# Activation rows of 272 instead of 266 floats in a float32r matmul stream: one inference step of a hybrid decoder trunk

## The chip, the cores and the metric

The kernel runs on one core of one Trainium2 chip. The metric is the device time of one execution in microseconds (us). A single profiled execution of the kernel before is at hand, and all durations of single instructions come from it.

## The reference

One decoding step of a two-layer trunk of width 2048 runs for 256 prompt tokens and 8 sample tokens together, 264 columns in all. Layer 0 mixes tokens by causal pooling over windows of 2, 4, 8 and 16; layer 1 by gated linear attention with four heads. Each mixer and each MLP ends in a layer norm over the residual:

```
x = layer_norm(alpha * x + mixer(x))          # pooling in layer 0, gated linear attention in layer 1
h = square(relu(x @ w1 + b1))                 # 2048 -> 8192
x = layer_norm(alpha * x + (h @ w2 + b2))     # 8192 -> 2048
...
proj = x @ w_in                               # layer 1: k, q, v and output gate, 48 blocks of 128 columns
y = (o * rsqrt(mean(o * o)) * norm_w * silu(og)) @ w_out
```

Outputs are the two groups' rows after the second layer, and the new pooling and attention states. All data are float32.

## The kernel before, in words

Activations lie transposed: 128 features on the partitions, and 264 tokens (`N`) along the free axis, so that the 2048 features make 16 tiles (`KT`). For accuracy, each float32 activation and each weight is split into a high part, rounded to the type float32r, and a low part, the rest. A product is then three float32r matmuls, issued by `mm3`: high weight by high activation (line 146), high weight by low activation (line 147), low weight by high activation (line 148). Two columns more (`NX` = 266) hold the gain and bias of a layer norm where a matmul takes them along, so that the norm can be applied after it.

The work is 320 units of weights: 128 for the MLP of each layer (four blocks, each of 16 units of `w1` and 16 of `w2`), 48 for `w_in`, 16 for `w_out`. A unit is a 128 x 2048 block of weights that gives one output tile. `stage` loads a unit by SP's DMA queue, two units ahead of its use; ScalarE casts it to the high part (line 133) and VectorE subtracts to get the low part (line 134). `project` then runs over the 16 activation tiles k, with three matmuls each, 48 in a row into one PSUM bank. TensorE's order is the program's order; between units small pieces of attention and norm work are slipped in by `slot`.

The activations of a stage are held by an object of the class `Parts`. Its 16 tiles are kept in eight pairs; a pair's high parts are one SBUF tile `hh` of 2 rows of `NX` floats in each partition, its low parts one tile `hl` of the same shape. Activation tile k is row k % 2 of pair k // 2. So `fresh` makes rows of 266 floats, 1,064 bytes, and hands out whole rows. Two sets of 16 such tiles exist, "a" and "b" (the method `hslot`); in the MLPs the stage of `w1` reads one and the stage of `w2` the other. In the compiled program of the kernel before the 32 slots lie 2,144 bytes apart (2 x 1,064, rounded up to a multiple of 32), from byte 38,912 of each partition on. In set "a" `hh` and `hl` slots alternate; in set "b" eight `hh` slots come before eight `hl` slots. The 128 x 128 weight blocks that the matmuls hold start at multiples of 512 bytes.

`Norm.__init__` lets GpSimd write the two extra columns (its lines 205 and 206 in the kernel before). In layer 1, head 0 has two tiles of its own, `k0` and `q0`, whose place is later taken by the high parts of the gated output of head 0; the other heads use slots of a set.

Of the kernel before, what the change touches and what calls it, by code (L numbers as in the profile page):

```python
# [6 lines left out]
F32 = mybir.dt.float32  # L7
F32R = mybir.dt.float32r
U8 = mybir.dt.uint8
AF = mybir.ActivationFunctionType  # L10
ALU = mybir.AluOpType
PSUM = bass.MemoryType.PSUM

P = 128
# [3 lines left out]
NS = 8  # L18
N = NP + NS
NX = N + 2  # L20
DFF = 8192
NBLK = DFF // D
HEADS = 4
# [28 lines left out]
def _body(ctx, tc, nc, a, o, stop):  # L52
    V, S, PE, G = nc.vector, nc.scalar, nc.tensor, nc.gpsimd
# [9 lines left out]
    def wtile():  # L63
        return work.tile([P, N], F32, name="wt")

    def bank(tag):
        return misc.tile([P, 512], F32, name=tag, bufs=2 if tag == "ma" else 1)
# [15 lines left out]
    def hslot(s, i, shape, dt, name):  # L83
        return hp.tile(shape, dt, name=name, tag=f"{s}{i}")

    class Parts:
        def __init__(self, s, pairs=range(8)):
            self.s = s
            self.hi, self.lo = [None] * KT, [None] * KT
            self.pairs = {}  # L90
            for i in pairs:
                self.fresh(i)

        def fresh(self, i, th=None):
            if th is None:
                th = hslot(self.s, i, [P, 2, NX], F32R, "hh")
            tl = hslot(self.s, 8 + i, [P, 2, NX], F32R, "hl")
            self.pairs[i] = th, tl
            for e in range(2):
                self.hi[2 * i + e], self.lo[2 * i + e] = th[:, e], tl[:, e]  # L100

        def pair(self, m):
            return self.pairs[m // 2]
# [34 lines left out]
    def next_unit():  # L138
        u = state["use"]
        state["use"] += 1  # L140
        while state["next"] < min(u + 1 + AHEAD, len(units)):
            stage()
        return ready.pop(u)
# [9 lines left out]
    def slot():  # L153
        for e in list(pending):
            e[0] -= 1
            if e[0] <= 0:
                pending.remove(e)
                e[1]()
        for chain in list(background):
            if next(chain, "done") == "done":  # L160
                background.remove(chain)
# [4 lines left out]
    def project(x, ncol=N):  # L166
        w = next_unit()
        ps = acc.tile([P, NX], F32, name="ps")
        for k in range(KT):
            c = slice((k % 8) * P, (k % 8 + 1) * P)  # L170
            hi, lo = w[k // 8]
            mm3(ps[:, :ncol], hi[:, c], lo[:, c], x.hi[k][:, :ncol], x.lo[k][:, :ncol], k == 0, k == KT - 1)
            if k % 4 == 3:
                slot()
        return ps
# [14 lines left out]
    class Norm:  # L190
        def __init__(self, name, x, ahead=1):
            self.g, self.b = name.replace("_", "_g"), name.replace("_", "_b")
            self.x = x
            self.ahead = ahead
            self.shifted = 8
            self.n = 0
            self.met = 0
            self.done = 0
            self.sd, self.sq, self.c = lnm, lnq, lnr
            if x is not None:  # L200
                at = OFF[self.g]
                gb = par[:, at:at + 2 * KT].rearrange("p (c m) -> p m c", c=2)
                for m in range(0, KT, 2):
                    hi, lo = x.pair(m)
                    G.tensor_copy(hi[:, :, N:], gb[:, m:m + 2])
                    G.tensor_tensor(lo[:, :, N:], gb[:, m:m + 2], hi[:, :, N:].bitcast(F32), op=ALU.subtract)

        def add(self, ps, scale=1.0):
            m = self.n
# [109 lines left out]
    def settle(ps, rows=P):  # L319
        col = work.tile([P, 2], F32, name="col")  # L320
        t = wtile()
        V.tensor_scalar(col[:rows], ps[:rows, N:NX], -1.0, None, ALU.mult)
        V.tensor_tensor(t[:rows], ps[:rows, :N], lnr[:rows], op=ALU.mult)
        V.scalar_tensor_tensor(t[:rows], lnm[:rows], col[:rows, 0:1], t[:rows], ALU.mult, ALU.add)
        return t[:rows], col[:rows, 1:2]

    def mlp(l, norm, x, h, nxt):
        later(2, norm.stats)
        for b in range(NBLK):
            for m in range(KT):  # L330
                bias = prm(f"b1_{l}", b * KT + m)
                if b == 0:
                    t, col = settle(project(x, NX))
                    V.tensor_tensor(col, bias, col, op=ALU.subtract)
# [23 lines left out]
    def gla(gctx, norm, xp, x, hg):  # L358
        gp = gctx.enter_context(tc.tile_pool(name="gp", bufs=1))
# [30 lines left out]
        def gate_low():  # L390
            ps = bank("mc")[:, :NX]
            for j in range(4):
                for e, part in enumerate((xp.hi, xp.lo)):
                    for g in range(4):
                        k = 4 * j + g
                        PE.matmul(ps[32 * g:32 * g + 32], lhsT=wg[:, 32 * k:32 * k + 32], rhs=part[k].bitcast(F32),
                                  start=j == 0 and e == 0, stop=j == 3 and e == 1, tile_position=(0, 32 * g))
            t, col = settle(ps)
            V.tensor_scalar(low, t, col, None, ALU.subtract)
# [24 lines left out]
        class Head:  # L424
            def __init__(self, h):
                self.h = h
                self.la = LA[:, 2 * h:2 * h + 2]
                self.pre = self.la[:, :, :NP]
                if h:
                    self.k = hslot(hg, 2 * h, [P, 2, N], F32, "k")  # L430
                    self.q = hslot(hg, 2 * h + 1, [P, 2, N], F32, "q")
                else:
                    self.k = gp.tile([P, 2, N], F32, name="k0")
                    self.q = gp.tile([P, 2, N], F32, name="q0")
                self.vtok = None
                self.oT = ZT[:, (8, 12, 0, 4)[h]:(8, 12, 0, 4)[h] + 4]
                self.turned = 0
                self.attended = self.sampled = self.normed = False
                self.lag = {}
# [256 lines left out]
        gated = Parts(hg, ())  # L696
# [23 lines left out]
        for h in range(HEADS):  # L720
            for t in range(4):
                ps = project(x)
                while not heads[h].normed:
                    slot()
                if t == 0:
                    for e in range(2):
                        gated.fresh(2 * h + e, gp.tile([P, 2, NX], F32R, name="kq"[e] + "0") if h == 0 else None)
                heads[h].gate(t, ps, gated)
        assert not background and not pending
        return gated  # L730
# [84 lines left out]
    with ExitStack() as gctx:  # L815
        xr = Parts("b")
        gated = gla(gctx, ln, ln.x, xr, "a")
        for m in range(KT):
            S.mul(Z[m], xr.hi[m][:, :N].bitcast(F32), ALPHA)
            V.scalar_tensor_tensor(Z[m], xr.lo[m][:, :N].bitcast(F32), ALPHA, Z[m], ALU.mult, ALU.add)  # L820
        xs = Parts("b")
        tc.keep_in_program_order(S.preload_act_table(AF.Abs_reciprocal_sqrt))
        ln = Norm("mix_1", xs)
        for m in range(KT):
            ln.add(project(gated))
# [10 lines left out]
def layout(i):  # L836
# [23 lines left out]
    tiles = lambda w, n: c(w.reshape(KT, P, n, P).transpose(2, 1, 0, 3)).reshape(n, P, D)  # L860
    r["w1"] = np.stack([tiles(w, DFF // P) for w in i["mlp_w1"]])
    r["w2"] = c(i["mlp_w2"].reshape(2, NBLK, KT, P, KT, P).transpose(0, 1, 4, 3, 2, 5)).reshape(2, NBLK, KT, P, D)
# [61 lines left out]
```

## Time and profile before

| | |
|---|---|
| median of 3 runs | 2081.34 us (2079.74 to 2082.94) |
| the profiled execution | 2082.59 us, of which its span from first to last instruction 2080.8 us |
| TensorE clock granted, mean over the span | 0.995 of 2.4 GHz |
| matmul records on TensorE | 16436, of them 15360 of `mm3` |

A row of the profile gives the line of the kernel, the engine (PE is TensorE, PEld its weight load, DVE VectorE, ACT ScalarE, POOL GpSimd, SP the queue of loads), the operation, the tiles written and read, shapes, count, busy time in us and the mean duration in ns. Matmuls overlap in the array, so the duration of one (285 ns) is longer than the distance between the starts of two. That distance, called pitch below, is what a row of matmuls costs.

### The profile page before, as it was taken

What the parts mean: (1) busy time and instruction counts of PE and PEld (TensorE: products, weight loads), DVE (VectorE), ACT (ScalarE), POOL (GpSimd) and SP (SyncE); (2) the same over time, 40 slices, a digit from 0 to 9 for tenths busy, and PEclk for the clock granted to TensorE, in tenths of its full rate; (3) what the DMA queues carried; (4) which work ended last, traced back from release to release, by engine and by line L of the source; (5) the groups of instructions that cost most, each with busy time, mean ns of one, the idle gap of its engine ahead of it and who ended that gap; (6) DMA issues with size and microseconds to landing.
All of it is one profiled execution on the core that took longest, in us unless ns stands there. A gap on an engine that the chain in (4) does not pass through costs nothing.

```text
span 2080.8 us, 38806 instructions
## 1 busy us (share of the span) xinstructions
PE 2055.9 (99%) x16436; PEld 2018.4 (97%) x16436; DVE 1254.3 (60%) x1969; ACT 1082.0 (52%) x1650; POOL 54.9 (3%) x130
## 2 busy tenths in 40 slices
PE   8999999999999999999999999999999999999996
PEld 8999999999999999998899999999999999999996
DVE  3976444444444458986778758865444444444465
ACT  3657355345435545856656645566454345435543
POOL 0000000000000000011111010000000000000000
PEclk9999999999999999999999999999999999999998
DMA  6554555554455554477676444545555455554442
GB/s 239 193 186 175 175 180 183 183 177 175 177 182 183 182 175 171 153 253 256 237 267 237 161 172 175 178 171 180 182 183 180 174 176 180 183 182 177 174 177 83
DMA packets 67470, 386.19 MB, mean 186 GB/s; under 512 B 7808, under 2 KB 12160, under 8 KB 25808
## 3 DMA queue, kind: packets, MB, share of 16 engines
q1 hardware_dynamic: 61232, 363.28, 49.9%
q0 software_dynamic: 5920, 20.28, 2.6%
q8 instruction: 128, 2.10, 0.4%
q14 instruction: 46, 0.38, 0.1%
q10 hardware_dynamic: 144, 0.16, 0.0%
HBM read 362.65 MB, written 22.14 MB: 185 GB/s over the span
## 4 chain that ended last, share of the span: by engine, by line
PE 94%; DVE 3%; ACT 1%; DMA 1%; SPq 0%; issue 0%; ACTq 0%; DVEq 0%
PE ps L146 30%; PE ps L148 30%; PE ps L147 30%; PE ma L469 1%; DVE wlo L134 1%; PE mb L638 1%; PE ma L567 1%; DMA xt<-in_xt 0%; PE ps L774 0%; ACT whi L133 0%; PE mc L624 0%; DMA raw<-in_w 0%; PE ma L523 0%; SPq L746 0%; DMA s<-in_st 0%
## 5 line engine op out<-in xcount | busy, mean ns | idle before, releaser
L147 PE MATMUL ps<-hl,whi 128*128 128x264 f32 (+1 forms) x5120 | 1460.7, 285 | 0.0
L146 PE MATMUL ps<-hh,whi 128*128 128x264 f32 (+1 forms) x5056 | 1454.0, 288 | 0.0
L148 PE MATMUL ps<-hh,wlo 128*128 128x264 f32 (+1 forms) x5056 | 1443.1, 285 | 0.0
L134 DVE TENSOR_TENSOR wlo<-raw,whi 128x1024 fp32r<-128x1024 f32 x640 | 783.5, 1224 | 606.9 <-ACT whi L133 604.6
L133 ACT CAST whi<-raw 128x1024 fp32r<-128x1024 f32 x640 | 671.0, 1049 | 857.9 <-PE ps L147 832.6
L147 PEld LDWEIGHTS ps<-hl,whi 128*128 128x128 f32 x5120 | 968.7, 189 | 3.7 <-issue 1.4
L146 PEld LDWEIGHTS ps<-hh,whi 128*128 128x128 f32 x5056 | 953.7, 189 | 16.5 <-issue 15.8
L148 PEld LDWEIGHTS ps<-hh,wlo 128*128 128x128 f32 x5056 | 955.4, 189 | 0.0
L179 DVE TENSOR_TENSOR hl<-wt,hh 128x264 fp32r<-128x264 f32 x188 | 79.9, 431 | 15.5 <-ACT hh L178 9.8
L350 DVE TENSOR_TENSOR zt<-zt,ps 128x264 f32<-128x264 f32 x96 | 41.2, 429 | 65.7 <-PE ps L148 65.6
L178 ACT CAST hh<-wt 128x264 fp32r<-128x264 f32 x188 | 76.7, 410 | 7.4 <-DVE wt L661 3.2
L339 ACT ACTIVATE wt<-wt 128x264 f32<-128x264 f32 x128 | 54.4, 425 | 3.9
L627 DVE SCALAR_TENSOR_TENSOR s<-mc,k,s 128x512 f32<-128x512 f32 x64 | 45.8, 744 | 3.4 <-PE mc L624 3.4
L338 ACT ACTIVATE wt<-ps,par 128x264 f32<-128x264 f32 x96 | 45.6, 475 | 0.0
L211 DVE SCALAR_TENSOR_TENSOR zt<-ps,zt 128x264 f32<-128x264 f32 x48 | 20.7, 431 | 38.9 <-PE ps L148 38.9
L607 ACT ACTIVATE s<-s,sa 128x512 f32<-128x512 f32 x64 | 42.7, 713 | 2.6 <-DMA s<-in_st 2.6
L628 POOL DMA_DIRECT2D out_ngs<-s x64 | 34.7, 542 | 351.0 <-DVE s L627 343.3
L253 ACT ACTIVATE wt<-zt 128x264 f32<-128x264 f32 x60 | 23.4, 411 | 17.0 <-DVE zt L211 17.0
L774 PE MATMUL ps<-px,pw 128*128 128x264 f32 x128 | 30.9, 402 | 0.0
L774 PEld LDWEIGHTS ps<-px,pw 128*128 128x128 f32 x128 | 25.3, 200 | 4.4
L302 ACT ACTIVATE wt<-zt,par 128x264 f32<-128x264 f32 x48 | 27.4, 601 | 1.1 <-DVE zt L301 1.1
L246 ACT ACTIVATE hh<-zt,par 128x264 fp32r<-128x264 f32 x48 | 24.1, 511 | 5.6 <-DVE zt L237 3.6
(181 smaller groups left out, 897.3 us busy)
## 6 DMA issues: line engine op xcount, KB each, us to landing
raw<-in_w SPq DMA_DIRECT2D x256, 1024.0 KB, 4.8
raw<-in_win SPq DMA_DIRECT2D x48, 1024.0 KB, 5.0
s<-in_st SPq DMA_DIRECT2D x64, 256.0 KB, 5.5
out_ngs<-s POOLq DMA_DIRECT2D x64, 256.0 KB, 3.0
raw<-in_wout SPq DMA_DIRECT2D x16, 1024.0 KB, 4.8
pw<-in_pw SPq DMA_DIRECT2D x4, 1024.0 KB, 9.9
xt<-in_xt SPq DMA_DIRECT2D x3, 768.0 KB, 8.8
out_y<-zt SPq DMA_DIRECT2D x8, 264.0 KB, 2.2
```

Source lines behind the costliest of these rows:

```text
L133: S.copy(hi, src)
L134: V.tensor_tensor(lo, src, hi.bitcast(F32), op=ALU.subtract)
L146: PE.matmul(ps, lhsT=whi, rhs=xh, start=start, stop=False)
L147: PE.matmul(ps, lhsT=whi, rhs=xl, start=False, stop=False)
L148: PE.matmul(ps, lhsT=wlo, rhs=xh, start=False, stop=stop_)
L178: S.copy(x.hi[m][:, :N], src)
L179: V.tensor_tensor(x.lo[m][:, :N], src, x.hi[m][:, :N].bitcast(F32), op=ALU.subtract)
L338: S.activation(t, project(x)[:, :N], AF.Relu, bias=bias)
L339: S.activation(t, t, AF.Square)
L607: S.mul(s0s[b][hf], s0s[b][hf], sa[:, 2 * h + hf, b:b + 1])
L627: V.scalar_tensor_tensor(s0, vb, self.k[:, hf, NP + b:NP + b + 1], s0, ALU.mult, ALU.add)
L774: PE.matmul(ps[:, :N], lhsT=w[:, c], rhs=px[2 * g + k // 2][:, k % 2], start=k == 0, stop=k == 3)
```

## The change

Rows of the pair tiles get 272 floats (1,088 bytes) instead of 266 (1,064), and the first 266 of each are used as before. The same is done to the two tiles of head 0, as `k0` and `q0` and as high parts of the gated output. No instruction is added or removed, and all shapes of reads and writes stay; only addresses change.

```diff
+NROW = 272
...
         def fresh(self, i, th=None):
             if th is None:
-                th = hslot(self.s, i, [P, 2, NX], F32R, "hh")
-            tl = hslot(self.s, 8 + i, [P, 2, NX], F32R, "hl")
+                th = hslot(self.s, i, [P, 2, NROW], F32R, "hh")
+            tl = hslot(self.s, 8 + i, [P, 2, NROW], F32R, "hl")
             self.pairs[i] = th, tl
             for e in range(2):
-                self.hi[2 * i + e], self.lo[2 * i + e] = th[:, e], tl[:, e]
+                self.hi[2 * i + e], self.lo[2 * i + e] = th[:, e, :NX], tl[:, e, :NX]
...
-                    G.tensor_copy(hi[:, :, N:], gb[:, m:m + 2])
-                    G.tensor_tensor(lo[:, :, N:], gb[:, m:m + 2], hi[:, :, N:].bitcast(F32), op=ALU.subtract)
+                    G.tensor_copy(hi[:, :, N:NX], gb[:, m:m + 2])
+                    G.tensor_tensor(lo[:, :, N:NX], gb[:, m:m + 2], hi[:, :, N:NX].bitcast(F32), op=ALU.subtract)
...
-                    self.k = gp.tile([P, 2, N], F32, name="k0")
-                    self.q = gp.tile([P, 2, N], F32, name="q0")
+                    self.k = gp.tile([P, 2, NROW], F32, name="k0")[:, :, :N]
+                    self.q = gp.tile([P, 2, NROW], F32, name="q0")[:, :, :N]
...
-                        gated.fresh(2 * h + e, gp.tile([P, 2, NX], F32R, name="kq"[e] + "0") if h == 0 else None)
+                        gated.fresh(2 * h + e, gp.tile([P, 2, NROW], F32R, name="kq"[e] + "0") if h == 0 else None)
```

## Rows read from the trace of the kernel before

**Rows 1.** The page's busy times: us, share of the span, instructions.

```profile
PE 2055.9 (99%) x16436; PEld 2018.4 (97%) x16436; DVE 1254.3 (60%) x1969; ACT 1082.0 (52%) x1650; POOL 54.9 (3%) x130
```

**Rows 2.** The chain that ended last, shares of the span by engine and line.

```profile
PE 94%; DVE 3%; ACT 1%; DMA 1%; SPq 0%; issue 0%; ACTq 0%; DVEq 0%
PE ps L146 30%; PE ps L148 30%; PE ps L147 30%; PE ma L469 1%; DVE wlo L134 1%; PE mb L638 1%; PE ma L567 1%; DMA xt<-in_xt 0%; PE ps L774 0%; ACT whi L133 0%; PE mc L624 0%; DMA raw<-in_w 0%; PE ma L523 0%; SPq L746 0%; DMA s<-in_st 0%
```

**Rows 3.** Busy time by stretch; the first lies inside the first MLP.

```profile
300.00:700.00 400.00, 400.00 (x3258) 400.00 (x3258) 195.20 (x204) 186.01 (x243) 0.00 (x0) 1.00 0.51 179
...
900.00:1100.00 200.00, 199.41 (x1544) 181.25 (x1544) 148.34 (x313) 121.11 (x213) 27.63 (x51) 1.00 0.74 258
```

**Rows 4.** TensorE's groups, shapes kept apart (the columns are the page's).

```profile
L147 PE MATMUL ps<-hl,whi 128*128 128x264 f32 x4480 | 1277.7, 285 | 0.0
L146 PE MATMUL ps<-hh,whi 128*128 128x264 f32 x4416 | 1268.5, 287 | 0.0
...
L146 PE MATMUL ps<-hh,whi 128*128 128x266 f32 x640 | 185.5, 290 | 0.0
...
L146 PE MATMUL ps<-q,whi 128*128 128x264 f32 x32 | 9.2, 287 | 0.0
```

**Rows 5.** Timeline of TensorE, a unit of 264 columns, line 147, tiles k = 0 to 8.

```profile
297.36 0.28 PE L147 MATMUL ps<-hl,whi 128*128 128x264 f32 x1
...
297.72 0.29 PE L147 MATMUL ps<-hl,whi 128*128 128x264 f32 x1
...
298.10 0.28 PE L147 MATMUL ps<-hl,whi 128*128 128x264 f32 x1
...
298.47 0.28 PE L147 MATMUL ps<-hl,whi 128*128 128x264 f32 x1
...
298.84 0.29 PE L147 MATMUL ps<-hl,whi 128*128 128x264 f32 x1
...
299.20 0.28 PE L147 MATMUL ps<-hl,whi 128*128 128x264 f32 x1
...
299.57 0.28 PE L147 MATMUL ps<-hl,whi 128*128 128x264 f32 x1
...
299.94 0.28 PE L147 MATMUL ps<-hl,whi 128*128 128x264 f32 x1
...
300.31 0.28 PE L147 MATMUL ps<-hl,whi 128*128 128x264 f32 x1
```

**Rows 6.** The same for a unit of 266 columns, k = 0 to 6.

```profile
1346.67 0.29 PE L147 MATMUL ps<-hl,whi 128*128 128x266 f32 x1
...
1347.05 0.28 PE L147 MATMUL ps<-hl,whi 128*128 128x266 f32 x1
...
1347.41 0.29 PE L147 MATMUL ps<-hl,whi 128*128 128x266 f32 x1
...
1347.78 0.29 PE L147 MATMUL ps<-hl,whi 128*128 128x266 f32 x1
...
1348.16 0.28 PE L147 MATMUL ps<-hl,whi 128*128 128x266 f32 x1
...
1348.53 0.28 PE L147 MATMUL ps<-hl,whi 128*128 128x266 f32 x1
...
1348.90 0.29 PE L147 MATMUL ps<-hl,whi 128*128 128x266 f32 x1
```

**Rows 7.** One line of `mm3` over the whole run: count, shortest/median/longest, first and last start.

```profile
L147 PE MATMUL ps<-hl,whi x5120: 278/285/389, 64.3 to 2061.5; 128*128 128x264 f32 x173, 128*128 128x266 f32 x24
```

**Rows 8.** The page's groups that write the pair tiles, and its loads of weights.

```profile
L179 DVE TENSOR_TENSOR hl<-wt,hh 128x264 fp32r<-128x264 f32 x188 | 79.9, 431 | 15.5 <-ACT hh L178 9.8
...
L178 ACT CAST hh<-wt 128x264 fp32r<-128x264 f32 x188 | 76.7, 410 | 7.4 <-DVE wt L661 3.2
...
raw<-in_w SPq DMA_DIRECT2D x256, 1024.0 KB, 4.8
```

## The prediction

> **What bounds the kernel now.** I read the page's busy times first, for which engine could set the end: TensorE is busy for 99% of the span, VectorE for 60%, ScalarE for 52%, GpSimd for 3% [rows 1]. The chain of work that ended last says the same from the other side: 94% of it is TensorE, and lines 146, 147 and 148, the three matmuls of `mm3`, hold 30% each [rows 2]. Then the stretches, to see whether any part of the run is bound otherwise. Inside the first MLP TensorE has no idle time at all in 400 us, while VectorE works 195 and ScalarE 186 of them; in attention, where the other engines have most to do, VectorE reaches 148 of 200 us and TensorE still stands at 199.4 [rows 3]. So the time is the pitch of TensorE's matmuls, from start to start, times their number. In the first MLP that is 400 us / 3258 = 122.8 ns [rows 3]. The granted clock there is 1.00, which is 2.4 GHz, so 264 columns at one column a cycle would take 110 ns. Some 12.8 ns of each pitch, a tenth of the run, is something else, and the change can only act there: it adds no instruction, it moves operands.
>
> **What the addresses are.** A row of 1,064 bytes is 66.5 times 16. A pair tile starts at a multiple of 32, so activation tile k starts on a multiple of 16 where k is even and 8 bytes past one where k is odd. With 1,088 bytes (17 times 64) and slots of 2,176 (34 times 64) from byte 38,912 (a multiple of 64), every row of every pair starts at a multiple of 64. If the address matters to TensorE, even and odd k must already differ in pitch.
>
> They do. The timeline shows line 147 once for each k, so two successive starts span three matmuls [rows 5]. From even k to odd k the four distances are 0.36, 0.37, 0.36 and 0.37 us, mean 365.0 ns; from odd to even 0.38, 0.37, 0.37 and 0.37, mean 372.5 ns. A distance of the first kind holds the pitches that follow the three matmuls of an even row (lines 147 and 148 of that k, and line 146 of the next, each right behind one that read an even row); the second kind holds those behind an odd row. The starts are rounded to 10 ns, so I averaged all pitches of the stream, first and last start and count per line as in [rows 7], leaving out the 206 of 135 ns and more, where other work or a wait stands between, and a dozen at both ends. This gives 13,253 pitches at 264 columns, mean 122.84 ns, and 1,888 at 266, mean 123.61. Sorted by the row that the matmul before had read, the 264-column pitches are 121.84 ns behind a multiple of 16 (6,716 of them) and 123.85 behind an odd row (6,537). The cost shows one instruction late.
>
> One suspicion has to be met: k also fixes which block of the weight tile is loaded, so the alternation could belong to the weights. The units of 266 columns say no. They load the same blocks, and there the order is reversed: even to odd 0.38, 0.37 and 0.37, odd to even 0.36, 0.38 and 0.37, means 373.3 and 370.0 [rows 6]; over all, 124.31 ns behind an even row (957) and 122.88 behind an odd one (931). The number of columns should not turn the sign of a weight effect. It does turn that of an effect of 16-byte pieces of the moving operand: 264 floats are 66 pieces from an even row and touch 67 from an odd one; 266 floats touch 67 either way, with the half piece at the end of an even row and at the front of an odd one.
>
> This is weighed against the Trainium skill. Its page Advanced Engine Details and Errata, section SBUF Cachelines, says that SBUF has lines of 16 bytes, and that accesses which stay in a line run at full rate while each new line costs. It gives no price; one line more is four columns, so an estimate from that page would be 4 / 2.4 = 1.67 ns for each odd row at 264 columns, half of 13,253 matmuls, 11 us saved, and nothing at 266 columns. The trace has 2.0 ns at 264 columns in that place, and at 266 a small loss.
>
> **The change part by part.**
>
> *Pair tiles as the moving operand of the 264-column matmuls.* There are 4,480 + 4,416 + 4,416 of these and four groups of 32 through head 0's tiles, 13,440 [rows 4]; 13,253 run at the plain pitch. Three readings of what an aligned stream costs:
> - behind any aligned row, 121.84 ns: 13,253 x 1.00 = 13.3 us saved;
> - where the row before and the matmul's own row are both multiples of 64 (1,216 cases), 121.46 ns: 13,253 x 1.38 = 18.3 us saved;
> - where the next row is one as well (608 cases, all line 147 in set "b"), 120.6 ns: 13,253 x 2.24 = 29.7 us saved.
> In the changed kernel all rows are multiples of 64, which speaks for the last. But those 608 cases come from four values of k alone, each with the same address three times in a row. I take the middle one, which includes them and has matmuls with a changing address beside them, and keep the outer two as bounds.
>
> *The 266-column matmuls.* 640 on each line [rows 4], 1,888 at the plain pitch. Behind aligned rows 124.31, where both rows are multiples of 64 124.02 (128 cases), with the next row too 123.62 (64), against 123.61 now. The same middle choice costs 1,888 x 0.41 = 0.8 us; the bounds are 1.3 and 0.
>
> *Writers of the tiles.* ScalarE's cast (line 178) and VectorE's subtraction (line 179) take 410 and 431 ns [rows 8]; parted into even and odd tiles both agree within 1 ns, so they neither gain nor lose. Even a few ns on 188 of each would lie in VectorE's idle half of an MLP [rows 3]. GpSimd's writes of the two extra columns keep their count and shape; only a step grows. GpSimd has 3% of the span to do [rows 1].
>
> *Space.* Each slot grows by 32 bytes, 1,024 for the 32 slots, and the two tiles of head 0 by 32 each. What lies behind moves by 1,024, so the weight blocks stay at multiples of 512. `k0` and `q0` get rows of 1,088 instead of 1,056, both multiples of 16; their own matmuls are a few dozen. I cost this at nothing.
>
> *What a quicker TensorE needs.* A unit of 48 matmuls takes 5.90 us now and would take 5.83. Its load lands 4.8 us after issue [rows 8] and is issued two units ahead, and its two casts and subtractions use about half of both engines. So no wait should take the place of what is saved.
>
> Sum: 18.3 - 0.8 = 17.5 us less. From the profiled execution of 2082.59 us (span 2080.8 and 1.8 around it) that is 2065.1. That execution stands 1.25 us above the median of 2081.34, so for the median I predict **2063.8 us**, 0.84% less. A difference of 0.2%, 4.2 us, is about what a measurement of this kernel can tell from none.
>
> **The rivals.**
>
> *Full alignment is worth its best case.* If the pitch falls to 120.6 and 123.62 everywhere, the time is 2081.3 - 29.7 = 2051.6. For it: the four values of k give nearly the same number there (120.0 to 121.2), while aligned rows at 32 past a multiple of 64 scatter. Against it: so few addresses.
>
> *Nothing moves.* The pitch could be set by the hand-over of weights: PEld is busy for all of the 400 us too [rows 3], and the alternation could be a shift of start times inside a period that stays as long as it is. Then 2081, within 4 us. Against it: the reversal at 266 columns, and the mean pitch that differs between 264 and 266 by 0.8 ns, as two columns at 2.4 GHz should, so the moving operand does set the length. The Trainium skill's page TensorE: Matmul & The Clock Gate, section Back-to-back issue gap, gives N / 2.4 + 2.5 ns for matmuls alone, 112.5 for 264 columns, and says that in a stream with weight loads both operations set the spacing; neither knows an address, so by that page nothing changes. The trace has 122.84, and even and odd rows apart.
>
> *Slower: equal residues collide.* Pitches also depend on the address in a wider period. In set "b", line 146 repeating its row's address on line 147 takes 126.9 ns at k = 0 and 126.7 at k = 4, but 120.1 at k = 8, and only the residue modulo 256 and the row before differ. After the change only the residues 0, 64, 128 and 192 are left, and weights stand at 0. If the first matmul of each k then paid 126.9 and the two others 121.84, the mean would be 123.5: 13,253 x 0.69 = 9.1 us more, with 1.3 at 266 columns 2091.8. It decides from a first pitch of 124.8 on, where the mean is back at 122.84. Against it: all four slow or mixed cases come behind an odd row, which no longer exists; and sorted by the residue of the row before, the four that stay have 121.53, 121.91, 122.18 and 122.16, all below the mean.
>
> **How the numbers follow.** The forecast (8 to 25 us less) has 0.56, the best case (more than 25) 0.16, a lesser gain between 4.2 and 8 us 0.07, nothing 0.13, slower 0.08. Faster by over 0.2% sums to 0.79. The range runs from 2047, a little below the best case, to 2080, inside the "nothing" case; outside lie the slower case, about 0.08 of "nothing" and 0.02 at the low end. The forecast's own range is 2056 to 2073.
>
> **What would show it.** In the stretch from 300 to 700 us the count of matmuls should rise from 3258 to about 3293 (400 / 0.12146), to 3283 by the weakest reading and 3317 by the strongest. Line 147's starts should be equally far apart from even and odd k. The 266-column units should be no quicker, pitch near 124.0. VectorE's and ScalarE's durations should stay at 431 and 410 ns. I am wrong if the alternation goes and the count stays, or if a fixed k still holds 126 ns and more.

## The result, and the profile after

The changed kernel takes 2062.99 us (median of 4 runs, 2061.60 to 2064.15); the kernel before, in the same comparison, 2082.14 us (4 runs, 2079.74 to 2084.03). The ratio is 0.9906, with a 95% interval of 0.9894 to 0.9918. The forecast was 2063.8 us.

The profiled execution after has a span of 2061.5 us against 2080.8, 19.3 us less. The busy times of the page, and the two stretches of [rows 3] again (us busy and count for TensorE, its weight loads, VectorE, ScalarE and GpSimd, then granted clock, DMA share and GB/s):

```profile
PE 2035.7 (99%) x16436; PEld 1998.2 (97%) x16436; DVE 1253.9 (61%) x1969; ACT 1084.5 (53%) x1650; POOL 54.9 (3%) x130
```

```profile
300.00:700.00 400.00, 400.00 (x3298) 400.00 (x3297) 198.04 (x207) 189.31 (x248) 0.00 (x0) 1.00 0.52 181
900.00:1100.00 200.00, 199.31 (x1544) 180.53 (x1537) 149.20 (x314) 125.07 (x218) 27.08 (x50) 1.00 0.73 255
```

TensorE is still never idle in the first stretch and has the same clock, but starts 3298 matmuls there instead of 3258: 400 / 3298 = 121.3 ns each instead of 122.8. The other engines have the work that they had. ScalarE and VectorE write the pair tiles at the same speed as in [rows 8], and weights land as late:

```profile
L180 DVE TENSOR_TENSOR hl<-wt,hh 128x264 fp32r<-128x264 f32 x188 | 80.0, 432 | 16.0 <-ACT hh L179 9.9
L179 ACT CAST hh<-wt 128x264 fp32r<-128x264 f32 x188 | 77.0, 412 | 7.5 <-DVE wt L662 3.3
...
raw<-in_w SPq DMA_DIRECT2D x256, 1024.0 KB, 4.8
```

The timeline of a unit of 264 columns answers to [rows 5]; the three lines of `mm3` are one further down in the changed kernel, so the low part's matmul is line 148:

```profile
295.17 0.28 PE L148 MATMUL ps<-hl,whi 128*128 128x264 f32 x1
...
295.53 0.28 PE L148 MATMUL ps<-hl,whi 128*128 128x264 f32 x1
...
295.89 0.28 PE L148 MATMUL ps<-hl,whi 128*128 128x264 f32 x1
...
296.26 0.28 PE L148 MATMUL ps<-hl,whi 128*128 128x264 f32 x1
...
296.62 0.28 PE L148 MATMUL ps<-hl,whi 128*128 128x264 f32 x1
...
296.98 0.28 PE L148 MATMUL ps<-hl,whi 128*128 128x264 f32 x1
...
297.35 0.28 PE L148 MATMUL ps<-hl,whi 128*128 128x264 f32 x1
...
297.71 0.28 PE L148 MATMUL ps<-hl,whi 128*128 128x264 f32 x1
...
298.07 0.28 PE L148 MATMUL ps<-hl,whi 128*128 128x264 f32 x1
```

From even to odd k the distances are 0.36, 0.37, 0.36 and 0.36 us, from odd to even 0.36, 0.36, 0.37 and 0.36: both means are 362.5 ns, where they were 365.0 and 372.5. In this unit the alternation is gone, and the odd rows have gained most. Over the whole trace a smaller one of the other sign is left: 121.66 ns behind even rows and 120.99 behind odd ones, where the prediction had 121.84 and 123.85. The same for 266 columns, beside [rows 6]:

```profile
1336.00 0.29 PE L148 MATMUL ps<-hl,whi 128*128 128x266 f32 x1
...
1336.37 0.29 PE L148 MATMUL ps<-hl,whi 128*128 128x266 f32 x1
...
1336.75 0.28 PE L148 MATMUL ps<-hl,whi 128*128 128x266 f32 x1
...
1337.12 0.29 PE L148 MATMUL ps<-hl,whi 128*128 128x266 f32 x1
...
1337.50 0.28 PE L148 MATMUL ps<-hl,whi 128*128 128x266 f32 x1
...
1337.86 0.29 PE L148 MATMUL ps<-hl,whi 128*128 128x266 f32 x1
...
1338.24 0.28 PE L148 MATMUL ps<-hl,whi 128*128 128x266 f32 x1
```

Six distances sum to 2.24 us, against 2.23 before: nothing gained. And here even and odd k do differ, 0.37, 0.37 and 0.36 against 0.38 each, although all rows start at a multiple of 64. A piece of 16 bytes cannot be the whole story.

Averaged over all starts as in the prediction (pitches of 135 ns and more left out), the pitch at 264 columns fell from 122.84 to 121.33 ns, and at 266 columns rose from 123.61 to 123.82. That is 13,253 x 1.51 = 20.0 us less and 1,888 x 0.21 = 0.4 us more, 19.6 in all, and the span has 19.3.

### The profile page after: what moved, and what is told of

Read it like the earlier page. It is cut to its first block, busy times and chain, and to the rows that moved or that the text cites. A ratio compares the mean times of both kernels' runs of the same rounds, so it can differ in the third digit from the quotient of the medians.

```text
span 2061.5 us, 38806 instructions
## 1 busy us (share of the span) xinstructions
PE 2035.7 (99%) x16436; PEld 1998.2 (97%) x16436; DVE 1253.9 (61%) x1969; ACT 1084.5 (53%) x1650; POOL 54.9 (3%) x130
## 4 chain that ended last, share of the span: by engine, by line
PE 94%; DVE 3%; ACT 1%; DMA 1%; SPq 0%; issue 0%; ACTq 0%; DVEq 0%
PE ps L147 30%; PE ps L148 30%; PE ps L149 30%; PE ma L470 1%; PE mb L639 1%; DVE wlo L135 1%; PE ma L568 1%; DMA xt<-in_xt 0%; PE ps L775 0%; PE mc L625 0%; ACT whi L134 0%; PE ma L524 0%; DMA raw<-in_w 0%; SPq L747 0%; ACT hh L247 0%
```

## The experiments

Three theories went into the first four runs. A: the moving operand is read in pieces of 16 bytes, and a row that starts off such a piece costs more. B: it must start at a multiple of 64. C: the slots' new places do it, or the move by 1,024 bytes of all tiles behind them. Diffs are against the changed kernel. The pitches below are averages over all starts of the run's own trace, by the same rule.

**Rows of 268 floats.**

```diff
-NROW = 272
+NROW = 268
```

> Rows of 268 floats (1,072 bytes, 67 times 16) in slots that stay 2,144 bytes apart, so no other tile moves and only the odd rows shift by 8 bytes. Theory A, pieces of 16 bytes: every row starts on a multiple of 16, so the whole gain comes: ratio to the kernel before 0.9906 within 0.002, pitch of the 264-column matmuls 121.3 ns, no difference between even and odd k. Theory B, a start at a multiple of 64 is needed: rows stand at 0, 48, 32 and 16 past a multiple of 64, one in four well placed as before: 2077 to 2082 us, pitch 122.5 to 122.8. Theory C, the places of the slots (starts at multiples of 64, or the 1,024 bytes by which all later tiles move) bring the gain: slots are those of before, so 2082 us.

Measured: 2064.71 us, ratio 0.9912 (0.9898 to 0.9926), pitch 121.53 ns. The slots are those of the kernel before; 8 bytes more on odd rows alone bring the gain. B and C fall. The stretch of [rows 3] counts

```profile
300.00:700.00 400.00, 400.00 (x3294) 400.00 (x3293) 197.67 (x207) 188.71 (x248) 0.00 (x0) 1.00 0.51 181
```

A difference between even and odd k remains, against what A said, but with the other sign: 121.87 ns for the matmuls of even k and 121.18 for those of odd k.

**Rows of 270 floats.**

```diff
-NROW = 272
+NROW = 270
```

> Rows of 270 floats (1,080 bytes, 67.5 times 16) in slots 2,176 bytes apart, those of the changed kernel; odd rows are again 8 bytes past a multiple of 16. Theory A: back to the kernel before, 2080 to 2084 us, pitches 121.8 behind even rows and 123.9 behind odd ones. Theory B: even rows stand at multiples of 64, odd ones do not: half the gain, about 2072 us. Theory C: the gain stays, 2063 us.

Measured: 2084.78 us, 1.0006 (0.9998 to 1.0015), pitch 123.06 ns. The slots of the changed kernel with odd rows 8 bytes off are worth nothing, as A says of the time:

```profile
300.00:700.00 400.00, 400.00 (x3251) 400.00 (x3250) 195.22 (x203) 185.41 (x244) 0.00 (x0) 1.00 0.51 179
```

The pitches by row did not come as expected: behind well placed rows 123.15 ns, behind badly placed ones 122.96, and not 121.8 and 123.9. Sorted by the row that a matmul reads itself, they are 122.38 and 123.74.

**All rows 8 bytes past a multiple of 16.**

```diff
-                self.hi[2 * i + e], self.lo[2 * i + e] = th[:, e, :NX], tl[:, e, :NX]
+                self.hi[2 * i + e], self.lo[2 * i + e] = th[:, e, 2:2 + NX], tl[:, e, 2:2 + NX]
...
-            return self.pairs[m // 2]
+            th, tl = self.pairs[m // 2]
+            return th[:, :, 2:2 + NX], tl[:, :, 2:2 + NX]
```

> Rows of 272 floats as in the changed kernel, but the 266 that are used begin 2 floats into the row, so that all rows, even and odd, start 8 bytes past a multiple of 16. Theory A: the cost is paid at every matmul instead of every second one. From the pitches before, 123.85 ns behind odd rows against a mean of 122.84, 13,253 x 1.01 = 13.4 us more, less 1,888 x 0.73 = 1.4 us at 266 columns: 2094 us, ratio 1.006; if the loss mirrors the gain, 2101 us. At 266 columns the pitch falls below the changed kernel's 123.8, to about 122.9. Theory B: no row at a multiple of 64, a little slower than before, under 2087 us. Theory C: 2063 us, slots and row spacing are those of the changed kernel.

Measured: 2090.93 us, 1.0037 (1.0024 to 1.0051). Slower than the kernel before and the changed one, and above the 2087 us of B, as only A says; but over the kernel before, 2082.92 us in the same comparison, it is 8 us and not 12 to 19. The pitch is 123.48 ns at 264 columns, and at 266 123.29, below the changed kernel's 123.82. The stretch of [rows 3] has:

```profile
300.00:700.00 400.00, 400.00 (x3241) 400.00 (x3241) 194.66 (x204) 184.79 (x241) 0.00 (x0) 1.00 0.51 178
```

So 2.15 ns lie between all rows on a piece's start (121.33) and all rows in the middle of one.

**Low parts alone.**

```diff
-NROW = 272
+NROW = 268
...
-                th = hslot(self.s, i, [P, 2, NROW], F32R, "hh")
+                th = hslot(self.s, i, [P, 2, NX], F32R, "hh")
...
-                        gated.fresh(2 * h + e, gp.tile([P, 2, NROW], F32R, name="kq"[e] + "0") if h == 0 else None)
+                        gated.fresh(2 * h + e, gp.tile([P, 2, NX], F32R, name="kq"[e] + "0") if h == 0 else None)
```

> Low parts in rows of 268 floats, high parts in rows of 266, slots 2,144 bytes apart as before. Of the three matmuls of a k only line 147 (here one line later) reads a low part, so rows that start 8 bytes past a multiple of 16 fall from three in six matmuls to two in six. Theory A: a third of the gain of 19 us, about 2075.5 us, ratio 0.997; the pitch falls behind the matmul that reads the low part of odd k alone, from 123.9 to about 121.5 ns. Theory B or C: 2081 to 2083 us.

Measured: 2083.10 us, 1.0000 (0.9992 to 1.0009), pitch 122.78 ns. A third of the gain was expected and nothing came; the pitch behind the low part of odd k, expected at 121.5 ns, is 122.6. Theory A does not hold matmul by matmul. I formed theory D from this: a change between a well and a badly placed row costs something as well, and this pattern has more changes.

**All rows 4 bytes past.**

```diff
-                self.hi[2 * i + e], self.lo[2 * i + e] = th[:, e, :NX], tl[:, e, :NX]
+                self.hi[2 * i + e], self.lo[2 * i + e] = th[:, e, 1:1 + NX], tl[:, e, 1:1 + NX]
...
-            return self.pairs[m // 2]
+            th, tl = self.pairs[m // 2]
+            return th[:, :, 1:1 + NX], tl[:, :, 1:1 + NX]
```

> All rows start 4 bytes past a multiple of 16 instead of 8. 264 floats still touch 67 pieces of 16 bytes, with 3 floats in the first and 1 in the last. If the count of pieces sets the price, the 264-column pitch is that of the run with all rows 8 past, 123.5 ns, and the time 2091 us. If it is the start address in pairs of floats, it is worse, over 124 ns and over 2095 us.

Measured: 2105.00 us, 1.0110 (1.0095 to 1.0125), pitch 124.54 ns; the stretch counts

```profile
300.00:700.00 400.00, 400.00 (x3212) 400.00 (x3211) 193.07 (x201) 182.41 (x239) 0.00 (x0) 1.00 0.50 177
```

This is 1.1 ns more than at 8 bytes past, with as many pieces touched. The count of pieces alone does not set the price. Whether the place inside the piece adds the rest, or the wider dependence on the address that the later runs show, is not told apart by this run.

**Well and badly placed rows in turn.** This run, and three later ones in its form, also write the two extra columns tile by tile, with 48 small GpSimd instructions more.

```diff
-                self.hi[2 * i + e], self.lo[2 * i + e] = th[:, e, :NX], tl[:, e, :NX]
+                k = 2 * i + e
+                fh, fl = (2, 0) if e else (0, 2)
+                self.hi[k], self.lo[k] = th[:, e, fh:fh + NX], tl[:, e, fl:fl + NX]
```

> Rows of 272 floats; in even k the low part starts 8 bytes past a multiple of 16, in odd k the high part, so that well and badly placed rows alternate at almost every matmul, half of them each as in the kernel before. If each badly placed row costs 2.1 ns by itself (121.4 with none, 123.5 with all): mean pitch 122.45, 2077 us. Theory D, that a change between the two kinds costs something as well (about 1.2 ns, from the kernel before, 122.84 with half badly placed and 2 changes in 6 matmuls, and the low-parts run, 122.78 with a third and 4 changes in 6): 123.65 ns, 2092 us.

Measured: 2077.16 us, 0.9974 (0.9963 to 0.9985), pitch 122.50 ns. Theory D falls: with a change at nearly every matmul the pitch is the mean of 121.4 and 123.5.

**The first half of k well placed, the second badly.** As above, with

```diff
+                fh, fl = (2, 2) if k >= 8 else (0, 0)
```

> Rows of 272 floats; the rows of k = 0 to 7 start on multiples of 16, those of k = 8 to 15 are 8 bytes past one. Half badly placed as in the kernel before, but only 2 changes of kind in 48 matmuls. Without a price of the change: 122.45 ns, 2077 us. Theory D: 121.4 + 1.05 + 0.05 = 122.5 ns, 2078 us, about 15 us less than with alternating rows. If instead any mixture costs what the kernel before costs: 122.84 ns, 2082 us.

Measured: 2079.21 us, 0.9985 (0.9975 to 0.9994), pitch 122.62 ns. Inside one execution the matmuls of k = 1 to 7 have 121.36 ns and those of k = 9 to 15 123.72; but for the 8 bytes, the rows of k and k + 8 stand in the same places modulo 512. The price follows the row's start.

**262 and 260 columns.** The two runs differ in one number:

```diff
+            n = {N: N - 2}.get(ncol, ncol) if 0 < k < KT - 1 else ncol
-            mm3(ps[:, :ncol], hi[:, c], lo[:, c], x.hi[k][:, :ncol], x.lo[k][:, :ncol], k == 0, k == KT - 1)
+            mm3(ps[:, :n], hi[:, c], lo[:, c], x.hi[k][:, :n], x.lo[k][:, :n], k == 0, k == KT - 1)
```

> The changed kernel, but in units of 264 columns the matmuls of k = 1 to 14 take only 262 columns; the last two sample tokens are left out of these sums. 262 floats are 65.5 pieces of 16 bytes, so 66 as with 264 floats. If a piece begun costs a whole one: pitch of these matmuls 121.3 ns and the time of the changed kernel, 2063 us. If columns count (1 / 2.4 GHz each): 120.5 ns, and 11,600 x 0.83 = 9.6 us less, 2053 us.

> As the run with 262 columns, with 260: four sample tokens are left out of the sums of k = 1 to 14. 260 floats are 65 whole pieces. If whole pieces count, at 1.84 ns each (121.3 / 66): 119.5 ns, and 11,600 x 1.84 = 21 us less than the changed kernel, 2042 us. By columns: 1.67 ns less, 2044 us; by the 262-column run, where two columns less gave 0.1 ns less, the step from 262 to 260 then holds 1.7 ns, more than twice what two columns are.

Measured: 2060.08 us and 2043.30 us (ratios 0.9893, 0.9877 to 0.9910, and 0.9811, 0.9796 to 0.9825). The shortened matmuls have 121.20 ns with 262 columns and 119.54 with 260, against 121.33 with 264. The stretch, first with 262 columns:

```profile
300.00:700.00 400.00, 400.00 (x3305) 400.00 (x3305) 197.90 (x207) 189.78 (x249) 0.00 (x0) 1.00 0.51 181
```

and with 260:

```profile
300.00:700.00 400.00, 400.00 (x3341) 400.00 (x3340) 200.58 (x209) 190.92 (x250) 0.00 (x0) 1.00 0.52 184
```

Two columns fewer, which leave a piece half used, give 0.13 ns; the next two, which drop the piece, give 1.66. For well placed rows a piece begun costs a whole one. Going up, the next two columns begin a 67th piece: in the changed kernel 266 columns take 123.82 ns against 121.33 with 264, 2.49 more.

**All rows 16 bytes past a multiple of 64.**

```diff
-                self.hi[2 * i + e], self.lo[2 * i + e] = th[:, e, :NX], tl[:, e, :NX]
+                self.hi[2 * i + e], self.lo[2 * i + e] = th[:, e, 4:4 + NX], tl[:, e, 4:4 + NX]
...
-            return self.pairs[m // 2]
+            th, tl = self.pairs[m // 2]
+            return th[:, :, 4:4 + NX], tl[:, :, 4:4 + NX]
```

> All rows of 272 floats start 16 bytes past a multiple of 64. Pieces of 16 bytes: 66 for 264 floats as in the changed kernel, pitch 121.3 to 121.5 ns, 2063 to 2065 us. If a multiple of 32 or 64 brings part of the gain: pitch over 121.8, time over 2069 us.

Measured: 2055.45 us, 0.9868 (0.9853 to 0.9883), pitch 120.82 ns:

```profile
300.00:700.00 400.00, 400.00 (x3312) 400.00 (x3310) 198.87 (x207) 189.68 (x250) 0.00 (x0) 1.00 0.51 182
```

No theory had this. It beats the kernel before and the changed kernel, and their intervals do not overlap.

**The two mixed patterns at other addresses.** The low-parts pattern and the pattern of the kernel before, both in rows of 272 floats, in the form of the alternating run. The first has

```diff
+                fh, fl = (2, 0) if e else (0, 0)
```

and the second

```diff
+                fh, fl = (2, 2) if e else (0, 0)
```

> The pattern of the low-parts run again (low parts on multiples of 16, high parts of odd k 8 bytes past one, a third of all rows badly placed), now in the slots of the changed kernel, 2,176 bytes apart. If the price goes by the share of badly placed rows (121.4 with none, 123.5 with all): 122.1 ns, 2073 us, and the 2083 us of the low-parts run came from its addresses in a wider period. If high parts alone set it, or the pattern does: 122.8 ns, 2082 us again.

> The pattern of the kernel before (both parts of odd k 8 bytes past a multiple of 16) in the slots of the changed kernel. By the share of badly placed rows: 122.45 ns, 2077 us. If the pattern sets the price: 122.84 ns, 2082 us. With rows of 270 the same pattern gave 123.06 ns at other addresses.

Measured: 2076.07 us, 0.9971 (0.9960 to 0.9982), pitch 122.43 ns; and 2084.66 us, 1.0011 (1.0001 to 1.0020), pitch 122.97 ns. The low-parts pattern, worth nothing at its first addresses, is 7 us quicker at the others. The pattern of even and odd k stays, in three arrangements (122.84, 123.06, 122.97), 0.4 to 0.6 ns above the mean of its two kinds.

## Why the prediction was right

**What bounds the kernel.** Right: in every run TensorE is busy for all 400 us of the stretch, the other engines have the same instructions (but for the 48 of GpSimd in four runs), and the time moved with the pitch of the matmuls.

**The address of the moving operand sets the pitch.** Right, and shown: the two halves of k in one execution, and 8 bytes more on the odd rows alone, which bring the time to 0.9912. The rival "nothing moves" falls by the same runs. So does what I drew from the Trainium skill's page TensorE: Matmul & The Clock Gate, section Back-to-back issue gap, that nothing changes because no address stands in its rule: the same matmuls had mean pitches between 120.8 and 124.5 ns by their rows' places alone.

**The size.** Of the three readings I took the middle, 121.46 ns and 18.3 us; measured are 121.33 and 20.0. The loss at 266 columns was put at 0.8 us and is 0.4. The sum of 17.5 us stands against 19.3 in the span. That 121.46 came so near is partly luck: three arrangements with all rows on multiples of 16 gave 120.82, 121.33 and 121.53 ns, and single places in the first MLP range from 115.9 to 127.3 in them. The best case, 120.6, did not come: in the first MLP of the changed kernel set "b" has 119.6 to 121.7 ns on the middle line of a k, by residue modulo 256, and 120.9 to 123.2 on the first.

**The line of 16 bytes.** I had weighed the section SBUF Cachelines of the Trainium skill's page Advanced Engine Details and Errata, with an estimate of 1.67 ns for a line more. A whole piece measured 1.79 ns (260 to 264 columns), a half-used one as much as a full one, so the trace agrees, for rows that start on a line, that a new line costs. The step from 264 to 266 columns, one piece more as well, is 2.49 ns. At 8 bytes past, where 264 floats touch one piece more, the 2.15 ns lie between these two, and 266 floats, which touch no further piece there, take no longer (123.29 against 123.48 ns); so the piece may be the whole price. At 4 bytes past it is 3.2 ns, more than one piece, and what adds the rest is not shown.

**"The cost shows one instruction late."** This step is not borne out. It sorted the kernel before well, but with all rows 8 bytes past the mean pitch by place in the pattern still runs from 121.7 to 126.3 ns, and in the low-parts pattern at its second addresses the slowest place, 124.2 ns, is behind a well placed row. With rows of 270 floats, the same pattern as in the kernel before, the sorting by the row before gives nearly nothing, 123.15 and 122.96. So the 121.84 and 123.85 from which I argued owed much to the addresses of that kernel: the step from "even and odd k differ" to "the start matters" was right in its end and lucky in its evidence. Single pitches carry a second, wider dependence; only means over many addresses show the first.

**The reversal at 266 columns.** I took it for the pieces' own sign. After the change even and odd k still differ there with all rows well placed, so the reversal was no clean proof, though the conclusion that the weights are not the cause stands by the rows of 268 floats, which left every weight in its place. The 0.8 ns between 264 and 266 columns, which I read as two columns at 2.4 GHz, were no sign of columns either: the difference is 2.49 ns in the changed kernel, and with all rows 8 bytes past 266 columns are 0.19 ns quicker than 264.

**The slower rival,** equal residues that collide, did not occur. But its ground, a dependence on the address in a wider period, is real: 16 bytes more on every row is worth another 7.5 us, and the low-parts pattern differs by 7 us between two sets of addresses. Where all rows start on multiples of 16, the traces show this period: 256 bytes. In the first MLP of the changed kernel the mean pitch of each of the three matmuls of a k repeats with every second k in set "a" and with every fourth in set "b", within 0.4 ns, and runs from 119.5 to 123.7 ns in between. The addresses agree modulo 256 at just these distances, while the blocks of weights come in the same order for both sets. With rows of 268 floats the addresses agree at every eighth k in set "a", where the pitch repeats within 0.5 ns, and not in set "b", where k and k + 8 differ by up to 9 ns. With all rows 8 bytes past, the pitch repeats where addresses agree modulo 512, and modulo 256 it does not: the second matmul of a k in set "a" has 127.8 ns at k = 4, 130.5 at k = 6 and 127.8 at k = 8. A row's own address does not decide alone: in the run with 16 bytes in front, the first and the third matmul of an even k in set "a" read the same row and take 115.9 and 123.3 ns. Whether rows meet each other, the weights or something else in this period stays open.

## What to carry to other kernels

When matmuls run back to back, look at the start address of each moving operand, not only at its shape: here a row length of 266 floats put every second tile 8 bytes off a multiple of 16 and cost 1% of the run. Sort the starts in the timeline by operand before building anything; a difference between even and odd tiles is visible in nine rows. It is a hint and no proof, and its absence proves nothing: by the row that they read themselves, the matmuls of even and odd k have 123.46 and 123.51 ns with all rows 8 bytes past, and 120.07 and 121.58 in the quickest run with all 264 columns, where every row starts on a multiple of 16. Then try a few paddings and offsets that are multiples of 16 bytes, since two that look alike can differ by 0.4%, as 272 floats with and without 16 bytes in front did. In the first MLP of the run with 16 bytes in front, single places run from 115.9 to 125.9 ns, so choosing addresses modulo 256 may gain more; no run here tried it.

## What the hardware showed unexpectedly

Moving a row's start by 16 bytes, from a multiple of 64, made the stream quicker (121.33 to 120.82 ns). Starts at 4 bytes past a multiple of 16 cost more than those at 8 (124.54 against 123.48 ns) with as many pieces touched. And 262 float32r columns take as long as 264 (121.20 and 121.33 ns), 260 clearly less (119.54). With all rows on multiples of 16, the pitch of a single matmul repeats with the address modulo 256 and differs by up to 10 ns between places (115.9 to 125.9 ns with 16 bytes in front).
